# Dilated attention heads: queries and keys kept whole in float32, two heads scored in the row halves of the array, and a first layer that begins with half a modulation chunk

## The chip, the cores and the metric

The kernel runs on one core of a Trainium2 chip. A core has five engines with their own instruction lists: TensorE (matrix products; PE in the profile, its weight loads PEld), VectorE (DVE), ScalarE (ACT), GpSimd (POOL) and SyncE (SP), which here issues all DMA transfers. The time is the device time of the whole program in microseconds (us); three runs of the kernel before took 1956.06, 1959.04 and 1960.41 us, so the median is 1959.04 us.

## What is computed

A two-layer encoder is applied to two groups of tokens, "p" with 512 and "s" with 1024 tokens of width 1024, all in float32. Every layer is RMSNorm, modulation by a shift and a scale that are computed from a conditioning vector, a mixer, RMSNorm, a gate and the residual sum:

```
shift, scale, gate = split(silu(c) @ ada_w + ada_b, 3)
h = rmsnorm(x, pre_g) * (1 + scale) + shift
p = h @ w_in                  # qa ka va ga qb kb vb gb (layer 0)
y = rmsnorm(concat(oa * silu(ga), ob * silu(gb)) @ w_out, post_g)
x = x + gate * y
```

Layer 0 has 8 dense heads ("a") and 8 dilated heads ("b") of 64 channels. A dilated head attends in three patterns, (window, dilation) = (128, 1), (512, 4), (2048, 16), each a sliding window over tokens of one residue; the three outputs are mixed by the softmax of their log sums:

```
for window, dil in ((128, 1), (512, 4), (2048, 16)):
    o, lse = sliding_window(residues(q, dil), residues(k, dil), residues(v, dil), window // (2 * dil))
w = softmax(stack(lse)); out = sum(w * outs)
```

Layer 1 has neighbourhood attention ("c") and a Fourier mixer.

## The kernel before, in words

Tokens go in units of 512: unit 2 is group p, units 0 and 1 are group s. Layer 0 does all of p first, then s; the end of p's layer 0 and the start of its layer 1 are woven into s.

**The planner.** Nobody writes the order of instructions of an engine out by hand. The program states operations on tiles of named pools, with a number of buffers for each; a planner walks through them with a model of the times and puts on each engine, in program order as priority, what has its data and its buffers. The order that results is fixed. On the chip an engine waits at the instruction that is next, even if a later one could go.

**Products.** Projections split both operands into a rounded high part and a low part (hi and lo, type float32r) and add three products (`tok_gemm`, `chan_gemm`; L141 is the helper that issues them). Products of plain float32 are two instructions each in the profile. A product can use a part of the 128 x 128 array: `tile_position=(row, column)`.

**Queries and keys of layer 0.** `s2_0_unit` projects 256 columns at a time, applies the rotary embedding, transposes and spills. `spill_hl` (L399 to L403) writes a high part (ScalarE) and a low part (VectorE) to DRAM, for dense and dilated heads alike; the queries are scaled by 0.125.

**The dilated heads.** `attn_b` calls `attn_b_unit` for each head and each half of 512 queries. A head loads its keys with the high parts on partitions 0 to 63 and the low parts on 64 to 127 (`load_k`, one buffer), and its queries' high and low parts, each copied to both halves (`load_q`). GpSimd adds the two to a float32 query `qf` (L741). For each tile of 128 queries there are two sections of scores in one PSUM bank ("S", two banks): the band, two rounded products over all 128 rows (L141, tiles `qh`, `ql`; two pieces of 128 keys where the tile is the first or last of the group), and the four residue classes modulo 4, float32 products with 32 columns of the array for each class (L769, `qf`). Band and classes are issued for two query tiles before `softmax_b` masks, takes the maximum (L804 or L809), the exponential (L816), and scales (L819), into tiles "e" (four buffers of 1024 columns; a head uses two). Then the transposes, the copies to SBUF, the products with V (L633) and `fold`.

**The beginning.** `run` loads the modulation weights of 512 channels (`ada_w`, four tiles of 512 KB for a chunk), `adaln` multiplies them with the conditioning vector (L222; eight float32 products on 32 columns each), copies, transposes by four small products (`adt`) and adds the bias. The order is: chunk 2 (scale of channels 0 to 511), the four tiles of x of unit 2 and their norm, chunk 0 (shift of the same channels), the weights of job "kva", chunks 3 and 1. `s1_part` builds the modulated operand for 256 channels at a time. The first half of job "kva" (channels 0 to 511) is multiplied before chunks 3 and 1 are; the second half, and all of job "qa0", after them.

Of the kernel before, what the change touches and what calls it, by code (L numbers as in the profile page):

```python
# [18 lines left out]
P = 128  # L19
# [103 lines left out]
class Body:  # L123
# [80 lines left out]
    def ada_w(self, l, c, tag="x", slots=XB):  # L204
        aw = self.a["ada_w"][l].rearrange("(p j) e -> p j e", p=P)
        ws = []
        for j in range(0, KC, 2):
            ws.append(self.sb.tile([P, 2, 512], F32, tag=tag, name=f"aw{l}{c}{j}", bufs=slots))
            self.dma(ws[-1], aw[:, j:j + 2, c * 512:c * 512 + 512])
        return ws  # L210

# [16 lines left out]
    def adaln_end(self, l, c, parts, alloc=None):  # L228
# [14 lines left out]
        pt = (alloc or self.pD)(f"adt{l}{c}")[:, 0:8].rearrange("p (k g) -> p k g", g=2)  # L243
        for k in range(4):
            self.mm(pt[:, k], parts[:, k * P:(k + 1) * P], self.sel, True, True)
        ks = slice(4 * (c % 2), 4 * (c % 2) + 4)
        mod = self.mod[:, l, row, ks, :]
        nc.vector.tensor_add(mod, pt, self.adb[:, l, row, ks].unsqueeze(2).to_broadcast([P, 4, 2]))
        if row == 1:
            nc.vector.scalar_tensor_tensor(mod, mod, 1.0, self.adb[:, l, 2, ks].unsqueeze(2).to_broadcast([P, 4, 2]),  # L250
                                           op0=ALU.add, op1=ALU.mult)
# [95 lines left out]
    def load_w(self, src, name, dve=()):  # L347
# [5 lines left out]
        for c in range(KC // 2):  # L353
# [40 lines left out]
    def spill_hl(self, ps, dst, u, scale, nm, classes=False):  # L394
# [9 lines left out]
        if not classes:  # L404
            self.dma(dst[:, :, u * 512:(u + 1) * 512].rearrange("t p s -> p t s"), st)
            return
        for t in range(2):
            self.dma(dst[t].rearrange("p (r a) -> p r a", r=4)[:, :, P * u:P * u + P],
                     st[:, t].rearrange("p (r a) -> p r a", r=4))
# [62 lines left out]
    def scratch0(self):  # L472
        dr = self.dr
        self.qd, self.kd, self.vd, self.gd, self.md = {}, {}, {}, {}, {}
        for g in self.G:
            n = g.name
            for p in range(8):
                self.qd[0, n, p] = dr.tile([2, P, g.S], F32R, name=f"q0{n}{p}")
            for p in [0, 4, 5, 6, 7]:
                self.kd[0, n, p] = dr.tile([2, P, g.S], F32R, name=f"k0{n}{p}")  # L480
# [10 lines left out]
    def w_0(self, kind, u):  # L491
        base = dict(qa=0, kv=512, ga=768, qb=1280, kb=1792, vb=2304, gb=2816)
        c0 = base[kind[:2]] + (0 if kind == "kva" else 256 * int(kind[2]))
        return self.load_w(self.a["w_in_ab"][0][:, c0:c0 + 256], f"{kind}{u}", W0)
# [15 lines left out]
    def s2_0_unit(self, H, u, w, typ, q, nm):  # L510
# [12 lines left out]
        for jp in range(2):  # L523
            i = 4 * gu + 2 * jp
            ps = self.early.pop((typ, jp), None)
# [25 lines left out]
        def finish():  # L551
            for c in range(1 if typ == "kva" else 2):
# [9 lines left out]
                elif typ == "kb":  # L562
                    self.spill_hl(pt, self.kd[0, n, 4 + 2 * q + c], gu, 1.0, f"{nm}{c}", g.U > 1)
                else:
                    self.spill_hl(pt, self.qd[0, n, 2 * q + c + (4 if typ == "qb" else 0)], gu, 0.125, f"{nm}{c}")
# [139 lines left out]
    def attn_b(self, g, h, quad):  # L705
        for head in range(4 * quad, 4 * quad + 4):
            self.attn_b_unit(g, h, head)
# [23 lines left out]
    def attn_b_unit(self, g, h, head):  # L731
# [3 lines left out]
        pr, hh = 4 + head // 2, head % 2  # L735
        nm = f"b{n}{head}{h}"
# [5 lines left out]
        kf = km.bitcast(F32)  # L742
        if hh == 0:
            self.vt = self.load_vb(g, h, pr, nm)
        V1, V2 = [[t[:, i, HD * hh:HD * hh + HD] for t in ts for i in range(t.shape[1])] for ts in self.vt]
        k4 = km.rearrange("p (r a) -> p r a", r=4)
        es = [pool.tile([P, 1024], F32, tag="e", name=f"e{nm}{i}", bufs=EB) for i in range(2)]
        ev = []
        pss = []
        for t in range(4):  # L750
            tt = 4 * h + t
            qs = slice(t * P, (t + 1) * P)
            ps = self.pS(f"s{nm}{t}")
            pss.append(ps)

            if 0 < tt < NT - 1:
                a0 = 32 * tt - 16
                self.qk(ps[:, 0:256].rearrange("p (j r a) -> p j r a", j=2, r=4), (qh, ql), qs,
                        k4[:, :, a0:a0 + 64].rearrange("p r (j a) -> p j r a", a=32))
            else:  # L760
                for j in range(2):
                    a0 = min(max(32 * (tt + j) - 16, 0), nn - 32)
                    self.qk(ps[:, j * P:(j + 1) * P].rearrange("p (r a) -> p r a", r=4), (qh, ql), qs, k4[:, :, a0:a0 + 32])
            if t % 2 == 0:
                continue

            for t in (t - 1, t):
                for r in range(4):
                    nc.tensor.matmul(pss[t][32 * r:32 * r + 32, 256:256 + nn], qf[:, t * P + 32 * r:t * P + 32 * r + 32],  # L769
                                     kf[:, r * nn:(r + 1) * nn], start=False, stop=True, tile_position=(0, 32 * r),  # L770
                                     skip_group_check=True)
            for t in (t - 1, t):
                ev.append(self.softmax_b(g, pss[t], es[t // 2][:, (t % 2) * 512:(t % 2) * 512 + 256 + nn], 4 * h + t, f"{nm}{t}"))
        po = self.pO(f"o{nm}")

        for gi in range(2):
# [4 lines left out]
            for j, t, cnt, x in ((0, 0, 1, 0), (1, 0, 2, 1), (2, 1, 1, 3)):  # L781
                t += 2 * gi
                self.pv2(po[:, t * P:(t + cnt) * P], V1[2 * gi + j], ph[:, x * P:(x + cnt) * P], j if gi == 0 else 2 + j)
# [9 lines left out]
        of = self.fold(po, nm, view=lambda x: x.rearrange("p (t r a) -> p r t a", t=4, r=4))  # L793
        self.dma(self.md[0, n, pr][HD * hh:HD * hh + HD, 512 * h:512 * h + 512], of)
# [381 lines left out]
    def run(self):  # L1176
# [4 lines left out]
        with tc.tile_pool(name="l0", bufs=1) as self.l0:  # L1181
            H = [], []
            self.dma(self.adb, self.a["mod_b"])
            self.adaln(0, 2, self.ada_w(0, 2, "hl", HB))()
            xs = self.s1_norm(0, 2)
            ws = self.ada_w(0, 0, "hl", HB)
            self.pre["kva"] = self.w_0("kva", 2)
            w3, w1 = self.ada_w(0, 3, "hh", HB), self.ada_w(0, 1, "e", EB)
            self.adaln(0, 0, ws)()
            pts = {k: self.s1_transpose(0, 2, xs, k, f) for k, f in enumerate([self.pS] * SB + [self.pT] * TB)}  # L1190
            self.s1_part(0, 2, xs, H, 2, pts)

            for jp in range(2):
                ps = self.early["kva", jp] = self.pD(f"tkva2{jp}").rearrange("p (t c) -> p t c", t=2)
                self.tok_gemm(ps, H, self.pre["kva"], jp, 0, 4)
            pts = {k + 4: self.s1_transpose(0, 2, xs, k + 4, f) for k, f in enumerate([self.pS] * SB + [self.pT] * TB)}
            self.adaln(0, 3, w3, self.pO)()
            self.adaln(0, 1, w1, self.pO)()
            self.s1_part(0, 2, xs, H, 2, pts)
# [134 lines left out]
```

## Time and profile before

| | us |
|---|---|
| median of three runs (1956.06 to 1960.41) | 1959.04 |
| profiled execution | 1960.37 |
| its span, first to last instruction | 1958.6 |
| TensorE busy | 1892.0 (97%) |
| VectorE busy | 1207.7 (62%) |
| ScalarE busy | 925.5 (47%) |
| GpSimd busy | 625.8 (32%) |

Busy time is the union of an engine's instructions; matrix products overlap in their pipeline, so an instruction's duration is longer than its distance to the next, and the distance is what counts in a dense stretch. The span is cut into 40 slices on the page: TensorE is at 7 tenths in the first one and at 8 or more in all others, and 354.03 MB go through the DMA queues, 181 GB/s on the mean.

### The profile page before, as it was taken

The page shows a single profiled execution, that of the slowest core. Times are in us where ns is not written, and L with a number is a line of the kernel's source. Part 1 is how long each engine was busy: PE and PEld are TensorE (multiplying, and loading weights), DVE is VectorE, ACT ScalarE, POOL GpSimd, SP SyncE. Part 2 cuts the span into 40 slices and gives each one's busy share as a digit, 9 for nine tenths or more (in the row PEclk, how much of TensorE's full clock was granted, in tenths as well). Part 3 has the DMA queues.
Part 4 walks back from the last instruction along what each step waited for, and adds up shares of the span by engine and source line. Part 5 has one row for each costly group of instructions (what it writes and reads, how often), then busy time and mean ns, then how long its engine had stood idle before and what let it go on. Part 6 is the DMA issues. An engine that isn't in the chain of part 4 may idle for free.

```text
span 1958.6 us, 38066 instructions
## 1 busy us (share of the span) xinstructions
PE 1892.0 (97%) x13720; PEld 1630.5 (83%) x13720; DVE 1207.7 (62%) x3131; ACT 925.5 (47%) x2195; POOL 625.8 (32%) x558
## 2 busy tenths in 40 slices
PE   7999999999999999999999999899999999998998
PEld 3889778999999888888986767798887888887898
DVE  2788765354858666767765586564566544668643
ACT  3456544343356554565544454454554333445531
POOL 2832234255622121121111231344433323335320
PEclk8999999999999999999999999999999999999999
DMA  9655564567664432244455585654667664668643
GB/s 337 218 178 162 174 183 154 169 202 226 224 219 140 130 96 87 77 134 139 125 163 167 178 284 163 215 173 138 217 214 231 196 188 142 201 207 263 209 169 140
DMA packets 266493, 354.03 MB, mean 181 GB/s; under 512 B 26568, under 2 KB 173352, under 8 KB 266304
## 3 DMA queue, kind: packets, MB, share of 16 engines
q1 hardware_dynamic: 266304, 351.60, 56.8%
q8 instruction: 108, 1.77, 0.4%
q14 instruction: 81, 0.66, 0.1%
HBM read 263.36 MB, written 88.16 MB: 179 GB/s over the span
## 4 chain that ended last, share of the span: by engine, by line
PE 78%; DMA 9%; DVE 7%; issue 2%; POOL 2%; ACT 1%; SPq 1%; POOLq 0%; ACTq 0%; DVEq 0%
PE y L141 9%; PE c1q L141 5%; PE c1g L141 5%; PE c1k L141 5%; PE t1v L141 5%; PE tvb L141 4%; PE ggb L141 3%; PE gga L141 3%; PE sas L141 3%; PE oas L141 3%; PE ptas L145 3%; PE tqb L141 2%; PE tkb L141 2%; PE tqa L141 2%; PE tkva L141 2%
## 5 line engine op out<-in xcount | busy, mean ns | idle before, releaser
L141 PE MATMUL y<-who,hhm 128*128 128x256 f32 x768 | 218.1, 286 | 4.7 <-ACT hhm L842 4.6
L141 PE MATMUL y<-who,hlm 128*128 128x256 f32 x768 | 216.3, 285 | 3.7 <-DVE hlm L843 3.6
L141 PE MATMUL y<-wlo,hhm 128*128 128x256 f32 x768 | 217.0, 285 | 0.4 <-DVE wlo L358 0.4
L141 PEld LDWEIGHTS y<-who,hhm 128*128 128x128 f32 x768 | 146.1, 191 | 8.4 <-ACT hhm L842 5.7
L141 PEld LDWEIGHTS y<-who,hlm 128*128 128x128 f32 x768 | 146.0, 191 | 7.2 <-DVE hlm L843 5.0
L141 PEld LDWEIGHTS y<-wlo,hhm 128*128 128x128 f32 x768 | 145.9, 191 | 1.7 <-issue 1.0
L680 ACT ACTIVATE eas<-sas,nmas 128x512 f32<-128x512 f32 x128 | 86.9, 684 | 71.0 <-DVE nmas L676 71.0
L1034 POOL TENSOR_TENSOR bics<-TTcs,mkc 128x288 f32<-128x288 f32 (+1 forms) x72 | 65.6, 912 | 128.0 <-DVE mcs L1047 105.6
L617 DVE TENSOR_TENSOR ptlas<-ptas,pthas 128x512 fp32r<-128x512 f32 x128 | 85.6, 684 | 18.3 <-ACT pthas L615 18.0
L671 DVE TENSOR_REDUCE mxas<-sas 128x1 f32<-128x512 f32 x128 | 86.4, 683 | 11.6 <-PE sas L141 10.8
L358 POOL TENSOR_TENSOR wlo<-wso,who 128x512 fp32r<-128x512 f32 x40 | 54.3, 1360 | 98.6 <-ACT who L357 91.7
L615 ACT CAST pthas<-ptas 128x512 fp32r<-128x512 f32 x128 | 70.4, 591 | 32.1 <-PE ptas L145 26.6
L141 PE MATMUL t1v<-wh1v,hl 128*128 128x256 f32 x288 | 82.3, 286 | 0.0
L141 PE MATMUL t1v<-wh1v,hh 128*128 128x256 f32 x288 | 82.0, 285 | 0.0
L141 PE MATMUL t1v<-wl1v,hh 128*128 128x256 f32 x288 | 81.6, 283 | 0.0
L1052 ACT ACTIVATE ecs<-ecs,ngmcs 128x288 f32<-128x288 f32 (+1 forms) x96 | 54.7, 571 | 55.8 <-DVE ngmcs L1050 54.6
L145 PE MATMUL ptas<-ident,eas 128*128 128x128 f32 x512 | 77.1, 272 | 1.5 <-DVE ptlas L617 1.5
L865 ACT ACTIVATE ysq<-y 128x256 f32<-128x256 f32 x96 | 36.7, 383 | 85.2 <-PE y L141 70.0
L141 PE MATMUL oas<-ptlas,Vas 128*128 128x256 f32 x256 | 69.4, 297 | 1.1 <-DVE ptlas L617 1.1
L141 PE MATMUL oas<-pthas,Vas 128*128 128x256 f32 x256 | 69.1, 285 | 0.0
L357 ACT CAST who<-wso 128x512 fp32r<-128x512 f32 x80 | 48.8, 616 | 42.2 <-issue 15.4
L842 ACT CAST hhm<-og 128x512 fp32r<-128x512 f32 x48 | 29.7, 619 | 79.7 <-POOL og L841 44.1
(615 smaller groups left out, 6475.1 us busy)
## 6 DMA issues: line engine op xcount, KB each, us to landing
aw<-ada_w SPq DMA_DIRECT2D x48, 512.0 KB
wso<-w_out_ab SPq DMA_DIRECT2D x48, 256.0 KB
kcs<-k1s SPq DMA_DIRECT2D x24, 384.0 KB
kbs<-k0s SPq DMA_DIRECT2D x16, 512.0 KB
wso<-w_out_cd SPq DMA_DIRECT2D x32, 256.0 KB
ws1k<-w_in_cd SPq DMA_DIRECT2D x28, 256.0 KB
wskb<-w_in_ab SPq DMA_DIRECT2D x24, 256.0 KB
wsqb<-w_in_ab SPq DMA_DIRECT2D x24, 256.0 KB
```

What stands on the lines that cost most here:

```text
L141: self.nc.tensor.matmul(out, l, r, start=start, stop=stop, skip_group_check=True)
L145: self.nc.tensor.transpose(out, in_, self.ident[:k, :k])
L357: nc.scalar.copy(hi, st)
L358: (nc.vector if c in dve else nc.gpsimd).tensor_sub(lo, st, hi)
L615: nc.scalar.copy(h[:rows, :w], pt[:rows, :w])
L617: nc.vector.tensor_sub(lo[:rows, :w], pt[:rows, :w], h[:rows, :w])
L671: nc.vector.tensor_reduce(mx[:, c:c + 1], ps, op=ALU.max, axis=AX.X, negate=True)
L680: nc.scalar.activation(e[:, 512 * c:512 * c + 512], pss[c], AF.Exp, bias=nmx, accum_out=den[:, c:c + 1])
L842: nc.scalar.copy(hh, t)
L865: nc.scalar.activation(sq[:, 0:256], ps[:, t], AF.Square, accum_out=ss[j][:, job:job + 1])
L1034: nc.gpsimd.tensor_add(b, T[:, :, wo:wo + w], self.mcol[:, kind, wo:wo + w].unsqueeze(1).to_broadcast([P, nrow, w]))
L1052: nc.scalar.activation(e, e, AF.Exp, bias=ngm, scale=0.125, accum_out=den)
```

## The change

**Dilated heads.** Their queries and keys are spilled as plain float32 by a new `spill` (one ScalarE operation, one DMA), into DRAM tiles of one part instead of two. `attn_b_unit` becomes `attn_b_pair`: two heads at a time. The keys of both heads are one tile, head 0 on partitions 0 to 63 and head 1 on 64 to 127, and so are the queries; `qf` and its addition are gone. For each query tile the band and the classes of both heads are float32 products over 64 rows, alternating between the heads (`HD * x` is the row); each head has its own S bank. The masks and exponentials of the two heads of a query tile follow its scores, and the pair holds four e tiles. What comes after the exponentials moves to `out_b`, unchanged.

**The beginning.** x is loaded first. `ada_w` can load half a chunk (256 channels, two tiles of 512 KB), and `ada_half` multiplies it. The order is: halves 0 of chunks 2 and 0, the first half of the weights of "kva" and "qa0", halves 1 of both chunks, chunks 3 and 1. After each half 256 channels of the operand are built, and both jobs "kva" and "qa0" multiply them, in four PSUM banks that stay theirs; the second half of their weights and of their products follows after chunks 3 and 1. The columns of the modulation are added in `ada_cols`, which was the end of `adaln_end`.

```diff
+    def ada_half(self, l, c, half, ws, alloc):
+        ps = alloc(f"ada{l}{c}{half}")[:, 0:256]
+        for j in range(KC):
+            q = 32 * (j % 4)
+            nc.tensor.matmul(ps[q:q + 32, :], self.sc[:, j, :], ws[j // 4][:, j % 4], start=(j < 4), stop=(j >= 4),
+                             tile_position=(0, q), skip_group_check=True)
+        parts = self.sb.tile([P, 512], F32, tag="scr", name=f"mod{l}{c}{half}", bufs=SCB)[:, 0:256]
+        nc.scalar.copy(parts, ps)
+        self.ada_cols(l, c // 2, 4 * (c % 2) + 2 * half, 2, parts, alloc)
...
+    def spill(self, ps, dst, u, scale, nm, classes=False):
+        st = self.sb.tile([P, 2, 512], F32, tag="sp", name="sp" + nm, bufs=SPB)[:, 0]
+        self.nc.scalar.mul(st, ps, scale)
+        if classes:
+            dst, st = (x.rearrange("p (r a) -> p r a", r=4) for x in (dst, st))
+            self.dma(dst[:, :, P * u:P * u + P], st)
+        else:
+            self.dma(dst[:, u * 512:(u + 1) * 512], st)
...
-    def attn_b_unit(self, g, h, head):
+    def attn_b_pair(self, g, h, pr):
-        km = self.load_k(self.kd[0, n, pr], HD * hh, S, nm)
-        qh, ql = self.load_q(self.qd[0, n, pr], HD * hh, h, nm)
-        qf = pool.tile([P, 512], F32, tag="qf", name="qf" + nm, bufs=1)
-        nc.gpsimd.tensor_add(qf, qh, ql)
+        km = pool.tile([P, S], F32, tag="k", name="k" + nm, bufs=KB)
+        self.dma(km, self.kd[0, n, pr])
+        q = pool.tile([P, 512], F32, tag="qh", name="q" + nm, bufs=QB)
+        self.dma(q, self.qd[0, n, pr][:, 512 * h:512 * h + 512])
-        es = [pool.tile([P, 1024], F32, tag="e", name=f"e{nm}{i}", bufs=EB) for i in range(2)]
+        es = [[pool.tile([P, 1024], F32, tag="e", name=f"e{nm}{x}{i}", bufs=EB) for x in range(2)] for i in range(2)]
+        rows = [slice(HD * x, HD * x + HD) for x in range(2)]
         for t in range(4):
+            pss = [self.pS(f"s{nm}{t}{x}") for x in range(2)]
...
+            for view, k in parts:
+                for x, rs in enumerate(rows):
+                    nc.tensor.matmul(view(pss[x]), q[rs, t * P:(t + 1) * P], k[rs], start=True, stop=False,
+                                     tile_position=(HD * x, 0), skip_group_check=True)
+            for r in range(4):
+                for x, rs in enumerate(rows):
+                    nc.tensor.matmul(pss[x][32 * r:32 * r + 32, 256:256 + nn], q[rs, t * P + 32 * r:t * P + 32 * r + 32],
+                                     km[rs, r * nn:(r + 1) * nn], start=False, stop=True, tile_position=(HD * x, 32 * r),
                                      skip_group_check=True)
+            for x in range(2):
+                ev[x].append(self.softmax_b(g, pss[x], es[t // 2][x][:, (t % 2) * 512:(t % 2) * 512 + 256 + nn], tt,
+                                            f"{nm}{t}{x}"))
+        for x in range(2):
+            v1, v2 = [[t[:, i, rows[x]] for t in ts for i in range(t.shape[1])] for ts in (V1, V2)]
+            self.out_b(g, h, pr, x, ev[x], v1, v2, f"{nm}{x}")
...
-            self.adaln(0, 2, self.ada_w(0, 2, "hl", HB))()
             xs = self.s1_norm(0, 2)
-            ws = self.ada_w(0, 0, "hl", HB)
-            self.pre["kva"] = self.w_0("kva", 2)
-            w3, w1 = self.ada_w(0, 3, "hh", HB), self.ada_w(0, 1, "e", EB)
-            self.adaln(0, 0, ws)()
...
+            wq = [self.ada_w(0, 2, "e", EB, 0), self.ada_w(0, 0, "e", EB, 0)]
+            weights(range(2))
+            wq += [self.ada_w(0, 2, [("sp", SPB)] * 2, half=1), self.ada_w(0, 0, [("sp", SPB), ("row", RB)], half=1)]
+            w3, w1 = self.ada_w(0, 3, "hh", HB), self.ada_w(0, 1, "hl", HB)
+            pts = {k: self.s1_transpose(0, 2, xs, k, self.pT) for k in range(2)}
+            ps = {(kind, jp): (self.pD if (kind, jp) != ("qa0", 1) else self.pO)(f"t{kind}2{jp}").rearrange(
+                "p (t c) -> p t c", t=2) for kind in W for jp in range(2)}
+            for c in range(2):
+                for i in range(2):
+                    self.ada_half(0, 2 - 2 * i, c, wq[2 * c + i], self.pS)
+                self.s1_part(0, 2, xs, H, 1, pts)
+                for (kind, jp), o in ps.items():
+                    self.tok_gemm(o, H, W[kind], jp, 2 * c, 2 * c + 2)
+                pts = {k: self.s1_transpose(0, 2, xs, k, self.pT) for k in (2 * c + 2, 2 * c + 3)}
+            weights(range(2, 4))
+            self.adaln(0, 3, w3, self.pS)()
+            self.adaln(0, 1, w1, self.pS)()
+            self.s1_part(0, 2, xs, H, 2, pts, alloc=(self.pT, self.pS))
```

## Rows read from the trace of the kernel before

**Rows 1.** The page's totals: busy us, share of span, instructions

```profile
PE 1892.0 (97%) x13720; PEld 1630.5 (83%) x13720; DVE 1207.7 (62%) x3131; ACT 925.5 (47%) x2195; POOL 625.8 (32%) x558
```

**Rows 2.** Busy time by stretch; last columns clock, DMA share, GB/s

```profile
0.00:50.00 50.00, 35.59 (x183) 18.80 (x184) 15.50 (x39) 15.74 (x34) 11.82 (x17) 0.85 0.95 336
...
196.00:309.00 113.00, 109.05 (x896) 84.66 (x894) 74.41 (x294) 53.54 (x121) 35.66 (x27) 0.97 0.55 166
990.00:1230.00 240.00, 235.62 (x1980) 175.46 (x1979) 162.22 (x430) 115.47 (x260) 53.33 (x40) 1.00 0.61 189
```

**Rows 3.** Busy time by stretch, score tiles sbs, then sbp (PE, PEld, DVE)

```profile
990.00:1230.00 240.00, 71.63 (x672) 37.22 (x672) 42.39 (x64) 1.00 0.61 189
...
196.00:309.00 113.00, 30.40 (x352) 20.58 (x352) 18.72 (x62) 0.97 0.55 166
```

**Rows 4.** TensorE's timeline, group s: start us, us, instruction, tiles

```profile
996.71 0.28 PE L141 MATMUL sbs<-kbs,qhbs 128*128 128x256 f32 x1
996.83 0.28 PE L141 MATMUL sbs<-kbs,qlbs 128*128 128x256 f32 x1
997.03 1.07 PE L769 MATMUL sbs<-kbs,qfbs 128*32 128x256 f32 x16
998.04 0.39 PE L141 MATMUL t1v<-wh1v,hl 128*128 128x256 f32 x1
```

**Rows 5.** The same, a second half of a head's work

```profile
1026.35 0.28 PE L141 MATMUL sbs<-kbs,qhbs 128*128 128x256 f32 x1
...
1026.68 0.63 PE L769 MATMUL sbs<-kbs,qfbs 128*32 128x256 f32 x6
1027.24 0.39 PE L141 MATMUL sbs<-kbs,qhbs 128*128 128x256 f32 x1
...
1027.67 1.05 PE L769 MATMUL sbs<-kbs,qfbs 128*32 128x256 f32 x10
```

**Rows 6.** The same, group p

```profile
260.67 0.65 PE L769 MATMUL sbp<-kbp,qfbp 128*32 128x128 f32 x16
261.25 0.66 PE L145 MATMUL pt1bp<-ident,ebp 128*128 128x128 f32 x4
```

**Rows 7.** TensorE's timeline, beginning; in brackets idle time and releaser

```profile
5.69 5.85 PE L222 MATMUL ada<-aw,sc 128*32 128x512 f32 x16 [5.69 <-DMA aw<-ada_w]
...
22.88 1.06 PE L222 MATMUL ada<-aw,sc 128*32 128x512 f32 x8
...
28.09 0.39 PE L141 MATMUL tkva<-whkva,hh 128*128 128x256 f32 x1
...
49.28 0.58 PE L141 MATMUL tkva<-whkva,hh 128*128 128x256 f32 x1 [1.59 <-DVE hh L316]
...
71.14 0.28 PE L141 MATMUL tqa<-whqa,hl 128*128 128x256 f32 x1
```

**Rows 8.** SyncE's queue, first modulation tiles; then busy time of a stretch

```profile
1.64 1.97 SPq L138 DMA_DIRECT2D aw<-ada_w  x4
...
5.00:10.00 5.00, 4.31 (x14) 0.78 (x16) 0.00 (x0) 0.00 (x0) 0.00 (x0) 1.00 1.06 402
```

**Rows 9.** Operations by tile: ns min/median/max, first and last start

```profile
L741 POOL TENSOR_TENSOR qfbs<-qhbs,qlbs x16: 1271/1295/1821, 962.6 to 1213.5; 128x512 f32<-128x512 f32 x16
...
L403 DVE SCALAR_TENSOR_TENSOR spqb<-qTqb,spqb x12: 675/681/692, 149.8 to 659.8; 128x512 fp32r<-128x512 f32 x12
...
L400 DVE TENSOR_TENSOR spkb<-qTkb,spkb x12: 675/681/693, 126.3 to 637.2; 128x512 fp32r<-128x512 f32 x12
```

**Rows 10.** Exponentials by tile; then a VectorE group of 990 to 1230 us

```profile
L816 ACT ACTIVATE ebs<-ebs,ngbs x64: 705/722/740, 994.7 to 1230.2; 128x512 f32<-128x512 f32 x64
...
L819 DVE TENSOR_SCALAR ebs<-ebs,rdbs x64: 462/486/1596, 995.7 to 1231.4; 128x512 f32<-128x512 f32 x64
L804 DVE CUSTOM_DVE_ANT_1 ebs<-sbs,mask_b x56: 675/688/693, 992.7 to 1227.4; 128x512 f32<-128x512 f32 x56
...
L627 DVE COPY ptc2bs<-pt2bs 128x512 f32<-128x512 f32 x15 | 10.3, 688 | 3.3 <-PE pt2bs L145 3.0
```

More of the change, by code (lines that the diff above doesn't have):

```diff
@@ L242, in adaln_end, with ada_cols @@
             return
[L243 to L244 removed]
+        self.ada_cols(l, row, 4 * (c % 2), 4, parts, alloc or self.pD)
+    def ada_cols(self, l, row, k0, nk, parts, alloc):
+        nc = self.nc
+        pt = alloc(f"adt{l}{row}{k0}")[:, 0:2 * nk].rearrange("p (k g) -> p k g", g=2)
+        for k in range(nk):
             self.mm(pt[:, k], parts[:, k * P:(k + 1) * P], self.sel, True, True)
[L246 removed]
+        ks = slice(k0, k0 + nk)
         mod = self.mod[:, l, row, ks, :]
[L248 removed]
+        nc.vector.tensor_add(mod, pt, self.adb[:, l, row, ks].unsqueeze(2).to_broadcast([P, nk, 2]))
         if row == 1:
[L250 removed]
+            nc.vector.scalar_tensor_tensor(mod, mod, 1.0, self.adb[:, l, 2, ks].unsqueeze(2).to_broadcast([P, nk, 2]),
                                            op0=ALU.add, op1=ALU.mult)
@@ L345, in w_pair, with load_w @@
         return [pool.tile(shape, F32R, tag=t, name=f"w{x}{name}", bufs=bufs) for x, t in zip("hl", tags)]
-    def load_w(self, src, name, dve=()):
+    def load_w(self, src, name, dve=(), cs=range(KC // 2)):
         nc, pool = self.nc, self.sb
@@ L352, in load_w @@
         his, los = [], []
-        for c in range(KC // 2):
+        for c in cs:
             st = pool.tile([P, 2, nc_], F32, tag="ws", name=f"ws{name}{c}", bufs=WSB)
@@ L403, in spill_hl @@
             nc.vector.scalar_tensor_tensor(st[:, 1], ps, scale, st[:, 0], op0=ALU.mult, op1=ALU.subtract)
[L404 to L409, printed above, removed]
+        self.dma(dst[:, :, u * 512:(u + 1) * 512].rearrange("t p s -> p t s"), st)
+    def spill(self, ps, dst, u, scale, nm, classes=False):
[6 more added lines that the diff above has]
+            self.dma(dst[:, u * 512:(u + 1) * 512], st)
     def spill_v(self, ps, nh, dst, nm):
@@ L476, in scratch0 @@
             n = g.name
-            for p in range(8):
+            for p in range(4):
                 self.qd[0, n, p] = dr.tile([2, P, g.S], F32R, name=f"q0{n}{p}")
-            for p in [0, 4, 5, 6, 7]:
-                self.kd[0, n, p] = dr.tile([2, P, g.S], F32R, name=f"k0{n}{p}")
+            self.kd[0, n, 0] = dr.tile([2, P, g.S], F32R, name=f"k0{n}0")
+            for p in range(4, 8):
+                self.qd[0, n, p] = dr.tile([P, g.S], F32, name=f"q0{n}{p}")
+                self.kd[0, n, p] = dr.tile([P, g.S], F32, name=f"k0{n}{p}")
             self.vd[0, n, "a"] = dr.tile([g.S, 2, P], F32R, name=f"va0{n}")
@@ L705, in attn_b @@
     def attn_b(self, g, h, quad):
-        for head in range(4 * quad, 4 * quad + 4):
-            self.attn_b_unit(g, h, head)
+        for pr in (4 + 2 * quad, 5 + 2 * quad):
+            self.attn_b_pair(g, h, pr)
     def load_vb(self, g, h, pr, nm):
@@ L1193, in run @@
[L1193 to L1199, printed above, removed]
+            W = {kind: ([], []) for kind in ("kva", "qa0")}
@@ new lines, in weights @@
+            def weights(cs):
+                for kind in W:
+                    if kind == "qa0":
+                        self.wend = [(("qh", "ql"), QB), (("pth", "ptl"), PTB)]
+                    for l, n in zip(W[kind], self.w_0(kind, 2, cs)):
+                        l += n
+                    self.wend = None
+            wq = [self.ada_w(0, 2, "e", EB, 0), self.ada_w(0, 0, "e", EB, 0)]
+            weights(range(2))
+            wq += [self.ada_w(0, 2, [("sp", SPB)] * 2, half=1), self.ada_w(0, 0, [("sp", SPB), ("row", RB)], half=1)]
```

69 lines of the change are left out of this document (31 added, 38 removed).

## The prediction

> **What bounds the kernel now.** I read the page's totals first, then busy time by stretch, then TensorE's timeline inside the two stretches that the change rewrites. TensorE is busy for 97% of the span [rows 1]. In the two stretches in which the dilated heads run it is busy 109.05 of 113 us and 235.62 of 240 us, while VectorE reaches about two thirds and GpSimd less than a third [rows 2]. Between the heads' own instructions stand products of other jobs (gates, projections, the output product), so a head's latency is filled, and the end comes when TensorE's list is done. What shortens that list shortens the run almost one for one; what relieves another engine or a queue is worth nothing until TensorE waits for it. The exception is the first 50 us: TensorE is busy there for only 35.59 us, at a mean granted clock of 0.85 of 2.4 GHz, while the DMA engines move 336 GB/s [rows 2].
>
> The sums are made against the profiled execution, 1960.37 us (span 1958.6 us and 1.8 us around it); the median of the runs is 1959.04 us, so I take 1.3 us off at the end.
>
> **The scores of the dilated heads.** All their score instructions keep TensorE busy for 71.6 us in the 1024-token group and 30.4 us in the 512-token group [rows 3]. There are 8 heads, 4 query tiles of 128 to a half, and 2 halves or 1: per query tile and pair of heads, 32 and 16 in number, that is 2.24 and 1.90 us. I count the change in such steps.
>
> Today a step has two sections. The banded scores are rounded products on the whole array, two (high and low query) for 256 keys; they follow each other at 0.12 us [rows 4]. The class scores are float32 products on 32 columns of the array each. Sixteen instructions, the eight products of two query tiles (a float32 product is two instructions), take 1.01 us at 256 keys and 0.58 us at 128 [rows 4, 6]. Four products on different columns thus run together, and I count waves: a wave is one instruction on each part of the array, 0.25 us for 256 columns and 0.145 us for 128. Changing the array's division costs about 0.1 us each way: 0.20 us between the last whole-array product and the first class product, where 0.12 is usual [rows 4].
>
> After the change both sections are float32 with 64 rows, head 0 on the upper rows, head 1 on the lower. No product in this trace is split by rows, so whether the halves run together as the column parts do has to be bounded.
> - Together everywhere: two waves of banded scores, two of class scores, two changes of division: 0.1 + 0.5 + 0.1 + 0.5 = 1.2 us a step (1.28 for the 8 edge steps, whose band is two pieces of 128 keys: four waves of 0.145). Small group: 0.1 + 0.5 + 0.1 + 0.29 = 0.99 us (edge 1.07). In all 24 x 1.2 + 8 x 1.28 + 8 x 0.99 + 8 x 1.07 = 55.5 us against 102.0: 46 us less.
> - Never together: each section twice, 2.4 and 2.56 us, 1.98 and 2.14 us: 111 us, 9 us more.
>
> Which end is nearer? Four column parts do run as one wave, and nothing in the rows sets rows apart from columns, so I take the hardware to do it. The order of instructions is what I doubt. Engines work in order, and the order was fixed by a planner that starts what has its buffers. There are two score banks. Today two query tiles share them; after the change the two heads of one tile do. The mask-and-maximum that empties a bank takes 0.69 us on VectorE [rows 10], so the second bank comes free that much after the first, and the planner lets the first proceed alone. That is already to be seen: in [rows 5] the first tile's band is followed by six class instructions (three products) before the second tile's band. I counted such a break in 12 of the 16 second halves of the heads' work in this group; the first halves, which find both banks free, are mostly whole, as in [rows 4]. After the change a break means that head 0's band and most of its class products go by without head 1: about two separate sections each, 2.44 and 2.06 us on average, no better than today. The first tile of each pair finds both banks free; of the other three I take three quarters to be broken, as today: 18 of 32 steps and 9 of 16. Then 14 x 1.22 + 18 x 2.44 = 61.0 us, and 7 x 1.03 + 9 x 2.06 = 25.7 us: 86.7 against 102.0, **15 us less**. With all of the other three broken it is 5 us less.
>
> The Trainium skill bears on the price of "together". "TensorE: Matmul & The Clock Gate", section Measured speedup vs the span model, gives 3.07 times for four row parts, so less than their number. The waves of four column parts here come nearer to four: 1.01 us for eight products of 2 x 256 columns [rows 4]. By the page's ratio, which I would put at 1.5 for two halves as an estimate, a paired step would cost about 1.6 instead of 1.2 us and the 15 us would be about 8; no run here shows a row part yet, and my sum goes by the waves.
>
> **What leaves other engines.** The sum that rebuilds the float32 query, 24 times 1.3 us on GpSimd, and 24 subtractions of 0.68 us on VectorE that made the low parts in the spill, go away [rows 9]. Keys are loaded once for a pair, queries once instead of four 64-row copies. All this lies beside a busy TensorE [rows 2]; I count it at nothing, with up to 5 us of gain (there is 4 us of idle TensorE in each of the two stretches) as the bound. Were that cover gone, 16 us of VectorE would be the most it is worth. What is late next is the tile of exponentials: a pair now holds all four, so the next pair's maximum waits until this pair's transposes have read them (the slow rival below).
>
> **The beginning.** TensorE starts at 5.69 us, 4.05 us after the first 512 KB were asked for [rows 7, 8], and the queue then moves 402 GB/s [rows 8], 1.3 us for each such tile. Today the order is 4 modulation tiles of 512 KB, 4 of x, 4 of modulation; the last modulation product of these ends at 23.9 us, and 4.15 us later, after its copy, transposes, additions, the modulated operand and its rounding, the first projection product starts at 28.09 us [rows 7]. After the change 4 tiles of x and 4 of half a modulation chunk suffice: the eighth lands at 5.7 + 7 x 1.3 = 14.8 us, its products take the 1.06 us of [rows 7], and 4.15 us later the first projection product starts, at 20.0: 8.1 us earlier. It is followed by 48 more products (of the first query job), which are taken off the later list, so they cost nothing. What is added is two more modulation products' worth of issue: four halves instead of two wholes, between 0 and 2 x 1.06 us; I take 1. The weights of the second projection job move ahead of mask and tables in the queue; they add 1 MB, 2.6 us, before the last modulations, which today lie landed while TensorE still works through the first products (those start their second half at 49.28 us [rows 7]; 12 MB at 402 GB/s are there by about 34 us). Gain **7 us**. Bounds: all 14.4 us of idle time of the first 50 us, or a loss of 3 us, if the first products find the low clock (0.85 on the mean in this stretch [rows 2]) for longer and the halves cost their full 2 us. The gain carries through, because TensorE is busy nearly all the time from there on.
>
> Sum: 1960.4 - 15 - 7 = 1938; against the median, **1937 us**.
>
> **The rivals.**
> - *Together everywhere.* If the planner puts both heads side by side in every step, 46 and 7 us go: 1907 us. For it: both heads' products stand next to each other in the program. Against: the breaks of [rows 5].
> - *The halves don't run together.* Then the change does not do what it says: 9 us more and 7 us less give 1962 us, within the measurement of no change. For it: no row of the trace shows a row split. The Trainium skill's page "TensorEngine Tiling (Array Packing)", section Key Properties, says that tiles are independent and that a change of division drains the engine; by that the halves run, and the drain is in my 0.1 us.
> - *Slower: four tiles of exponentials.* A pair holds all four, so pairs follow each other in a chain: four steps of 2 x (0.69 + 0.49) us on VectorE, 0.72 us for the last exponential, and eight copies of 0.69 us between the transposes [rows 10], 15.7 us at least. Today a pair's two heads take 240 / 8 = 30 us with what stands between [rows 2], so there is slack of about 14 us. It decides from the point at which waiting in queues doubles the chain, which VectorE at two thirds could do. At 34 us a pair, 8 pairs cost 32 us and 4 small ones some 12: with 7 us gained at the start 1960 + 44 - 7 = 1997 us; at 32 us it is about 1975. Against it: the other jobs' products fill such waits today.
>
> **Chances and range.** Forecast 0.6, with its own range of 1922 to 1952 (5 to 25 us from the scores, 3 to 12 from the start); together everywhere 0.15; halves not together 0.13; chain of exponentials 0.12. The range of 8 in 10 is 1904 to 1959: it takes in the forecast, the first rival down to 3 us beyond its time, and a part of the second. A measurement here tells about 0.2% (4 us) from no change. Faster: 0.6 + 0.15 + 0.03 of the third = 0.78; within 0.2%: 0.10; slower: 0.12.
>
> **What would show it.** Paired steps: float32 products of 64 rows in waves of 0.25 us, with head 0's and head 1's first instructions some hundredths of a microsecond apart; their busy time over both groups 55 us (together), about 87 (forecast) or about 111 (never). Broken steps: class products of one head between the bands of the two. The start: first projection product at about 20 us, end of the first query job some 7 us before today's 71.3 us [rows 7]. The chain: TensorE idle in front of score products that wait for VectorE, and a lower share in 990 to 1230 us. I am wrong in the mechanism if the score time falls and the end does not, or if the start gains more than the scores.

## The result and the profile after

The changed kernel takes 1942.49 us (median of 5 runs, 1940.53 to 1945.32), the kernel before beside it on the same chip 1957.11 us. The ratio is 0.9928, 95% interval 0.9907 to 0.9949: 14 us faster, 10 to 18 by the interval. The forecast was 1937 us, 22 less than before. The profiled execution took 1940.53 us (span 1938.7), 19.9 us less span than that of before. It is the fastest of the five, and the profiled one of before (1960.37 us) is among the slowest of its kind, so accounts from the two traces show some 5 us more than the times do.

The page's totals of the changed kernel, to be set beside [rows 1] (busy us, share of the span, instructions):

```profile
PE 1879.1 (97%) x13752; PEld 1624.4 (84%) x13752; DVE 1186.0 (61%) x3110; ACT 927.1 (48%) x2197; POOL 591.8 (31%) x534
```

Busy time by stretch of the changed kernel, with the columns of [rows 2]; the last two are the stretches from the first to the last score product of a dilated group:

```profile
0.00:50.00 50.00, 34.24 (x257) 24.45 (x257) 14.74 (x42) 19.06 (x40) 17.68 (x22) 0.99 0.92 303
188.00:293.00 105.00, 101.23 (x879) 77.13 (x878) 70.71 (x293) 50.96 (x116) 26.53 (x20) 0.98 0.45 130
968.00:1205.00 237.00, 235.99 (x1981) 171.85 (x1980) 156.80 (x426) 115.58 (x261) 33.02 (x25) 1.00 0.50 155
```

TensorE is still busy for 97%, and in group s for 235.99 of 237 us; GpSimd and the transfers fell and nothing took the room. The score products alone, busy time of TensorE, weight load and VectorE in two stretches that hold all of them (group p, then s), against [rows 3]:

```profile
150.00:330.00 180.00, 25.83 (x352) 13.93 (x352) 19.10 (x64) 0.99 0.47 141
```
```profile
950.00:1260.00 310.00, 64.72 (x672) 26.11 (x672) 42.50 (x64) 0.99 0.51 160
```

TensorE's timeline of the changed kernel, group s: first a whole step at 968.95 (an edge step, whose band is two pieces), the last line being the next job; then a broken one from 1001.03:

```profile
968.95 0.72 PE L791 MATMUL sbs<-kbs,qbs 64*128 64x128 f32 x8
969.60 0.66 PE L796 MATMUL sbs<-kbs,qbs 64*32 64x256 f32 x16
970.19 0.50 PE L141 MATMUL c1q<-hh,wh1q 128*128 128x512 f32 x1
...
1001.03 0.70 PE L791 MATMUL sbs<-kbs,qbs 64*128 64x256 f32 x2
1001.65 0.62 PE L796 MATMUL sbs<-kbs,qbs 64*32 64x256 f32 x4
1002.21 0.66 PE L662 MATMUL obs<-ptc2bs,V2bs 128*64 128x128 f32 x8
...
1003.82 0.70 PE L791 MATMUL sbs<-kbs,qbs 64*128 64x256 f32 x2
1004.44 0.65 PE L796 MATMUL sbs<-kbs,qbs 64*32 64x256 f32 x12
1005.02 0.39 PE L141 MATMUL t1v<-wh1v,hl 128*128 128x256 f32 x1
```

Whole: both heads' band and class products in 0.65 + 0.59 = 1.24 us. Broken: head 0's band and two of its class products in 1.18 us, and after another job head 1's band and the other six in 1.20 us. Sixteen class instructions of two heads took 0.59 us from their first start to the start of the next job, four took 0.56 and twelve 0.58: the length of such a stretch hardly depends on how many parts of the array work in it.

The busy time of a group of instructions says more than it costs: an instruction ends after the next one has started (0.66 us busy, 0.59 to the next start). For the accounts below I took from the trace, for each TensorE instruction, the time to the next one's start, at most its own length (its slot), and called the rest idle. In slots the scores of both groups fell from 94.8 to 85.9 us, and TensorE's idle time after the first product from 51.8 to 41.3. All slots together are the page's busy time, in which the overlaps are counted once: 1892.0 and 1879.1 us. The first product comes 3.3 us later.

The beginning of the changed kernel, TensorE's timeline (against [rows 7]):

```profile
8.99 0.69 PE L145 MATMUL xt<-ident,x 128*128 128x128 f32 x2 [8.99 <-DVE x L310]
...
11.69 1.08 PE L221 MATMUL ada<-aw,sc 128*32 128x256 f32 x8 [0.33 <-DMA aw<-ada_w]
...
18.63 1.02 PE L141 MATMUL adt<-sel,mod 128*128 128x2 f32 x4 [0.81 <-ACT mod L224]
20.81 1.08 PE L221 MATMUL ada<-aw,sc 128*32 128x256 f32 x8 [1.16 <-DMA aw<-ada_w]
21.82 1.97 PE L145 MATMUL xt<-ident,x 128*128 128x128 f32 x8
23.44 0.56 PE L141 MATMUL tkva<-whkva,hh 128*128 128x256 f32 x1
```

and, of the same kernel, ScalarE's rounding that makes the first operand:

```profile
20.80 0.62 ACT L340 CAST hh<-xm 128x512 fp32r<-128x512 f32 x1
```

The operand is there at 21.42 us. But a quarter chunk of the second half's modulation (the row of 20.81, for whose transfer TensorE waited 1.16 us) and eight transposes stand ahead of the projection in TensorE's order, so it starts at 23.44.

### The profile page after: what moved, and what is told of

It reads as the page before. It is cut to its first block, busy times and chain, and to the rows that moved or that the text cites. A ratio compares the mean times of both kernels' runs of the same rounds, so it can differ in the third digit from the quotient of the medians.

```text
span 1938.7 us, 37892 instructions
## 1 busy us (share of the span) xinstructions
PE 1879.1 (97%) x13752; PEld 1624.4 (84%) x13752; DVE 1186.0 (61%) x3110; ACT 927.1 (48%) x2197; POOL 591.8 (31%) x534
## 4 chain that ended last, share of the span: by engine, by line
PE 47%; DMA 4%; DVE 2%; issue 1%; ACT 0%; POOL 0%; SPq 0%; POOLq 0%; ACTq 0%; DVEq 0%
PE y L141 10%; PE t1v L141 5%; PE c1g L141 5%; PE c1q L141 5%; PE c1k L141 5%; PE ocs L662 2%; PE ptcs L145 2%; PE obs L662 2%; PE sbs L791 1%; PE sbs L796 1%; PE scs L141 1%; PE oas L141 1%; PE c1d L141 1%; DMA og<-g1s 1%; PE pt1bs L145 1%; PE ocp L662 1%
## 5 line engine op out<-in xcount | busy, mean ns | idle before, releaser
L644 ACT CAST pthas<-ptas 128x512 fp32r<-128x512 f32 x128 | 70.6, 590 | 29.2 <-PE ptas L145 25.7
L1086 ACT ACTIVATE ecs<-ecs,ngmcs 128x288 f32<-128x288 f32 (+1 forms) x96 | 54.7, 571 | 56.9 <-DVE ngmcs L1084 55.5
```

The source lines that it names most:

```text
L644: nc.scalar.copy(h[:rows, :w], pt[:rows, :w])
L1086: nc.scalar.activation(e, e, AF.Exp, bias=ngm, scale=0.125, accum_out=den)
```

## The experiments

Theory A, from the prediction: TensorE's list sets the end, a paired step costs 1.2 us and a broken one double, and each slot saved is saved from the time. Its rivals: the halves don't run together, or a chain of other engines sets the pace of the heads.

**1. The heads alone**, with the beginning of before:

```diff
-            wq = [self.ada_w(0, 2, "e", EB, 0), self.ada_w(0, 0, "e", EB, 0)]
-            weights(range(2))
...
+            self.adaln(0, 2, self.ada_w(0, 2, "hl", HB))()
             xs = self.s1_norm(0, 2)
+            ws = self.ada_w(0, 0, "hl", HB)
...
```

> The dilated heads of the changed kernel with the beginning of the kernel before. Theory A (TensorE's list of instructions is the bound, so its time is what counts): the score products fall from 94.8 us to 85.9 us of TensorE's time, by the distance from each to the next instruction in the two traces, so about 9 us less than before, and up to 5 more where a load or a subtraction that is gone held TensorE up: ratio to before 0.993 to 0.996. Theory B (what counts is the lighter load on the queue, VectorE and GpSimd): all of the gain of the changed kernel but the beginning's, also 7 to 13 us; this run alone does not part the two, the next two do. If the beginning made the whole gain, the ratio is 1.000.

Ratio 0.997 (0.9958 to 0.9983), by which it takes 5.9 us less than before. Score slots fell by 8.8 us; about 3 of them were lost again in slots of other products (the heads' own transposes +2.1, a query projection +1.8), and idle time stayed (51.8 to 51.1).

**2. The beginning alone**, with the heads of before (`attn_b_unit` and both parts of queries and keys):

```diff
-        for pr in (4 + 2 * quad, 5 + 2 * quad):
-            self.attn_b_pair(g, h, pr)
+        for head in range(4 * quad, 4 * quad + 4):
+            self.attn_b_unit(g, h, head)
...
```

> The beginning of the changed kernel with the dilated heads of the kernel before. Theory A: the modulation products take 6.1 us less of TensorE's time, and at equal amounts of TensorE work the changed kernel was 8.4 us ahead when the first dilated scores began, so 7 to 9 us less than before, ratio 0.9955. If the head start is given back later to a wait that does not move (the first keys' round trip through DRAM, the tables of the second group), the ratio is 0.998 to 1.000.

Ratio 0.9984 (0.9973 to 0.9995), by which it takes 3.1 us less, under the 7 to 9 expected. In its profile the first dilated score of group p comes at 188.4 us, 8.1 earlier than before, and the first one of group s at 982.2, 8.8 earlier, so the beginning gives what it was to give and the lead holds that far. The last score of s comes at 1221.5 us, only 4.7 earlier: between the two TensorE idles for 6.9 us instead of 4.4, and the same products take 1.6 us more in slots. By the end of the span 5.7 us are left. Why the lead shrinks there no run shows. The two parts alone add to 9.0 us, both together gave 14; the intervals (3.3 to 8.2, 1.0 to 5.3, 10 to 18) don't exclude that they simply add.

**3. Apart**: head 0's band and classes, then head 1's.

```diff
-            for view, k in parts:
-                for x, rs in enumerate(rows):
+            for x, rs in enumerate(rows):
+                for view, k in parts:
...
-            for r in range(4):
-                for x, rs in enumerate(rows):
+                for r in range(4):
```

> The changed kernel, but with the loop over the two heads outside: head 0's band and classes, then head 1's, so that no product of one row half has the other half beside it. Transfers, banks and the work on VectorE, ScalarE and GpSimd are the same. By the planned order there are 139 sections of scores in the larger group and 66 in the smaller, where the changed kernel has 103 and 49; at 0.63 us a band section, 0.56 and 0.34 us a class section that is 114 us instead of 86. Theory A: 28 us more than the changed kernel, about 1971 us, slower than the kernel before. Theory B: within 5 us of the changed kernel.

Ratio 1.0011 (0.9993 to 1.0029): 17 us slower than the changed kernel by the medians (1959.6), 23 by the spans. Its score products, TensorE busy time first, in the stretches of above:

```profile
150.00:330.00 180.00, 34.90 (x352) 18.61 (x352) 20.43 (x64) 0.97 0.44 129
```
```profile
950.00:1260.00 310.00, 85.91 (x672) 33.63 (x672) 44.04 (x64) 1.00 0.48 148
```

120.8 us against 90.6; in slots 115.6 against 85.9, where 114 was expected. One head's class products, eight instructions, take 0.57 us from start to next start, where sixteen of two heads took 0.59:

```profile
994.36 0.64 PE L794 MATMUL sbs<-kbs,qbs 64*32 64x256 f32 x8
994.93 0.70 PE L791 MATMUL sbs<-kbs,qbs 64*128 64x256 f32 x2
```

The same products in the same number cost 30 us more because they don't meet: the halves do run together. Of the 28 us that were expected in time, 17 came; some of the rest is seen elsewhere (idle time fell by 4.7 us, slots of the output product by 3.9). By Theory B, the lighter load on the queue, VectorE and GpSimd, this run would have stayed within 5 us of the changed kernel: it is out as the whole cause.

**4. Together**: after a query tile's softmax, VectorE rewrites one column of the next tile's query from 0 times the maximum of head 1. The next tile's scores so wait until both banks are read, and both heads start side by side.

```diff
+            if t < 3:
+                c = (t + 1) * P
+                nc.vector.scalar_tensor_tensor(q[:, c:c + 1], self.mxb, 0.0, q[:, c:c + 1], op0=ALU.mult, op1=ALU.add)
...
+        self.mxb = mx[:, 0:1]
```

> The changed kernel, but each query tile's scores of both heads wait for the maximum of both heads of the tile before: one small VectorE operation adds zero times that maximum to the first column of the next tile's queries (values unchanged). Then both score banks are free when the planner begins a tile, and it puts the heads side by side: 67 sections in the larger group and 37 in the smaller instead of 103 and 49, 59 us of TensorE's time instead of 86. Theory A: 27 us less than the changed kernel, about 1915 us. Theory B: no change, or a little slower by the 36 added operations. The rival of the four tiles of exponentials: the gain stays under 10 us, and TensorE shows idle time before score products that wait for VectorE.

Score slots fell as expected, by 25.6 us to 60.3. The time did not: ratio 0.9929 (0.9911 to 0.9948), the changed kernel's own. Idle time rose by 22.5 us to 63.8, and the slots of all other products by 7.6 (the output product's by 4.8). Busy time by stretch, the changed kernel (columns as in [rows 2]):

```profile
960.00:1080.00 120.00, 119.98 (x952) 88.29 (x950) 75.23 (x200) 55.94 (x122) 14.34 (x11) 1.00 0.45 137
1080.00:1160.00 80.00, 79.00 (x653) 56.11 (x651) 57.52 (x151) 42.11 (x95) 16.30 (x12) 1.00 0.64 205
1160.00:1260.00 100.00, 91.83 (x815) 79.02 (x813) 61.13 (x148) 46.67 (x124) 23.61 (x24) 0.97 0.51 162
```

and "together":

```profile
960.00:1080.00 120.00, 120.00 (x971) 90.36 (x970) 74.35 (x213) 58.01 (x126) 15.13 (x12) 1.00 0.46 142
1080.00:1160.00 80.00, 66.26 (x614) 51.59 (x612) 57.13 (x143) 37.89 (x90) 17.16 (x12) 0.94 0.63 200
1160.00:1260.00 100.00, 83.63 (x778) 72.14 (x775) 60.57 (x157) 44.58 (x113) 19.16 (x22) 0.90 0.47 147
```

Up to 1080 us nothing is lost: by the count of TensorE's instructions other than scores, "together" leads by 10.0 us at 1046 us, and by nothing at 1240. In between TensorE stands still, and its granted clock falls to 0.94 and 0.90 as well. TensorE's waits from 960 to 1260 us (us in total, times, longest), first the changed kernel's longest:

```profile
PE y L141 <- ACT hhm L876: 5.6, 1, 5.6
```

then those of "together", of which the last is the added wait itself:

```profile
PE y L141 <- ACT hhm L880: 14.2, 2, 10.0
PE sbs L791 <- DMA kbs<-k0s: 7.4, 3, 4.5
PE y L141 <- POOL wlo L378: 3.4, 1, 3.4
...
PE sbs L791 <- DVE qbs L804: 0.4, 1, 0.4
```

and two of them in its timeline:

```profile
1084.27 0.39 PE L141 MATMUL c1d<-hh,wl1d 128*128 128x512 f32 x1
1089.14 0.70 PE L791 MATMUL sbs<-kbs,qbs 64*128 64x256 f32 x4 [4.48 <-DMA kbs<-k0s]
...
1240.73 0.58 PE L141 MATMUL y<-who,hhm 128*128 128x256 f32 x1 [9.95 <-ACT hhm L880]
```

At 1084.27 us the last projection (c1d) that needs nothing of the heads has run; in the changed kernel all of these products (12.47 us of busy time) still lie between 1080 and 1120 us. From here on, as I read these waits, a pair's chain is bare: its keys, for which there is one place, then scores, softmax and outputs, and last the way of the outputs through memory to the operand of the output product. The tiles of exponentials are in this chain too. VectorE waits for the transposes to free them, in the changed kernel (first line) and in "together" (second); in the kernel before it has no such wait in this stretch:

```profile
DVE ebs L838 <- PE pt2bs L145: 12.1, 5, 4.3
DVE ebs L841 <- PE pt2bs L145: 15.2, 6, 3.6
```

In the changed kernel TensorE has other products for this time. Theory A held while there was something to fill with. I call the corrected one A': a saved slot is worth its time only as long as other products last.

**5. Together in group p alone.**

```diff
-            if t < 3:
+            if t < 3 and n == "p":
```

> The changed kernel with the wait of e4 (the next query tile's scores start only when both heads' sums of the tile before are read) in group p alone; group s scored as in the changed kernel. In the order of TensorE's instructions group p has 37 stretches of score products of one division in place of 49. Theory A (TensorE's list sets the end; what is saved is kept wherever other products are left to fill the waits): score slots of p 24.6 to about 19.0 us as in e4, idle time of TensorE within 2 us of the changed kernel's 41.3, time 4 to 6 us under the changed kernel's, ratio to the kernel before 0.9900 to 0.9910. Rival (the added wait gives back in p too what it saves): ratio 0.9925 to 0.9935, idle time up by 4 us or more.

Ratio 0.9884 (0.9862 to 0.9905), 1936.36 us, 6.1 us under the changed kernel by the medians (3.6 by the profiled executions). Slots of p fell by 5.6 us, idle time rose by 2.5. In group p, where over 600 us of other work follow before the next dilated head, the slots are kept.

**6. Together in p and in the first half of s.**

```diff
-            if t < 3:
+            if t < 3 and h == 0:
```

> The wait of e4 in group p and in the first half of group s's queries (the first 16 of its 32 query tiles of a pair of heads); the second half as in the changed kernel. Stretches of one division: 37 in p (49), 87 in s (103). Theory A' (TensorE's list bounds until the other products run out, about two thirds into group s's attention; after that the chain of key load, scores, exponentials and output does): score slots 85.9 to about 71, and because the second half is not slowed the idle time rises by under 6 us, not by 22 as in e4; time 8 to 14 us under the changed kernel's, 1929 to 1935, ratio 0.986 to 0.989. Rival (the work left to fill is used up earlier by just as much, so the loss comes back in the second half): idle time up by 10 us or more, ratio 0.991 to 0.994.

Ratio 0.989 (0.987 to 0.991), 1937.25 us: no better than 5, though the score slots are 9.0 us fewer than there. Idle time rose from 43.8 to 49.9, and what opened lies between 1080 and 1160 us again (first line, TensorE busy for 72.02 of 80 us); its waits, same view as in 4:

```profile
1080.00:1160.00 80.00, 72.02 (x621) 51.98 (x620) 56.79 (x141) 36.99 (x87) 14.28 (x11) 0.94 0.59 191
...
PE y L141 <- ACT hhm L880: 9.2, 2, 6.2
PE sbs L791 <- DMA kbs<-k0s: 5.0, 2, 4.3
```

Neither side's numbers were met in full: idle time rose by 8.6 us against the changed kernel, where A' had under 6 and the rival 10 or more; the ratio is at the edge of A', the time outside it. Against 5, the 9.0 us of score slots came back as 6.1 us of idle time and 3.1 us in other products' slots. So for s the rival has the better of it: what is saved early in s uses up the filling products earlier, and is paid back.

**7. Experiment 4 with a second place for the keys of s.**

```diff
-        km = pool.tile([P, S], F32, tag="k", name="k" + nm, bufs=KB)
+        if n == "s" and pr % 2 == 0:
+            km = self.l0.tile([P, S], F32, tag="rope", name="k" + nm, bufs=1)
+        else:
+            km = pool.tile([P, S], F32, tag="k", name="k" + nm, bufs=KB)
```

> e4 (the wait in both groups) with a second place for the keys of group s's pairs, so that a pair's keys load while the pair before is scored. Stretches of one division in s: 77 (67 in e4, 103 in the changed kernel). Theory A' (in e4's last third the key load of about 5 us a pair stands open on TensorE): the 7.4 us that score products of s waited for keys in e4 are gone, idle time 63.8 to 52 to 57, score slots up by about 5 us against e4's 60.3, time 1936 to 1941, ratio 0.989 to 0.992. Rival (the chain through VectorE, exponentials and output is the slow one and the key load lies beside it): idle time within 3 us of 63.8, time as e4 or slower, ratio 0.992 to 0.996.

Ratio 0.9918 (0.9897 to 0.9938), 1942.88 us, not to be told from 4. The waits for keys are gone and idle time is 57.1, just above the 52 to 57 of A'. But the score slots are 67.8 us, 7.5 more than in 4 where about 5 were expected, and that takes the 6.7 us of idle time back. The next links are late too, in the same view:

```profile
PE y L141 <- ACT hhm L883: 11.7, 2, 10.3
PE sbs L794 <- DVE mxbs L844: 4.9, 3, 2.8
PE y L141 <- POOL wlo L378: 4.2, 1, 4.2
```

Score products now wait for the maximum, the output product as before. So the key load was one link of the chain, and to remove it brought nothing, in part because the second place changes the order of the scores as well (77 stretches of one division in s for 67). That the key load alone held the end, as my part of A' had it, is not shown.

**8. The second place for keys alone**, in the changed kernel: the diff of 7 without that of 4.

> The changed kernel with a second place for the keys of group s's pairs and no added wait. Stretches of one division in s: 116 in place of 103, because one pair's products now also stand between the other's. Theory A (TensorE's list bounds here): the earlier keys buy nothing, the 13 stretches more cost 13 by 0.58 us, score slots up by 7 to 8 us, time 5 to 8 us over the changed kernel's, ratio 0.9955 to 0.997. Rival (the key loads of the 8 pairs bound group s's attention in the changed kernel too): time 5 us or more under it, ratio below 0.990.

Ratio 0.9952 (0.9936 to 0.9968), 1949.16 us: 6.7 us slower than the changed kernel by the medians (all five runs lie above its five, though the two intervals overlap) for 7.4 us more of score slots. Keys earlier bought nothing; a second pair's products between the first pair's broke more steps.

**9. Together in p and in the first two pair passes of s.**

```diff
-            if t < 3:
+            if t < 3 and (n == "p" or (h == 0 and pr < 6)):
```

> The wait of e4 in group p and in the first two of the eight pair passes of group s (two of four pairs, first half of the queries), which lie before the stretch where idle time opened in e4 and e6. Stretches of one division in s: 95 (103 in the changed kernel, 87 in e6). Theory A' (saved slots are kept while other products fill the waits, and what is used up early is missing in the last third): score slots of s fall by another 4 us against e5's; if the fill lasts, the time is 4 us under e5's 1936, 1930 to 1934, ratio to the kernel before 0.985 to 0.9875, idle time within 2 us of e5's 43.8. Rival (every wait added in s is paid back in the last third, however early it stands, because the same filling products are then missing there): time 1935 to 1939, idle time up by 3 us or more against e5's.

Ratio 0.9861 (0.9841 to 0.988), 1934.05 us, the fastest median, and with 5 faster than both kernels. Idle time is 44.7 us, within 2 us of that of 5, as A' had it. Against 5 it is not settled: the intervals overlap, the profiled span is 1 us longer (1935.8), and 2.9 us of score slots saved in s stand against 2.7 more in the output product.

## Why the prediction came out as it did

**The bound** was read rightly for the changed kernel and too simply for what lies beyond it. Where slots were added (experiments 3 and 8) or saved in p (5), time followed, by 0.6 to 1.1 us for each; the 25.6 us of experiment 4 brought nothing. That was my own sign of a wrong mechanism, the score time falling and the end not; for the change itself experiment 1 has both falling.

**The price of a step** is right: 1.24 us for the whole edge step shown where I had 1.28, 2.38 in the two halves of a broken one where I had 2.44. So is the share of broken steps: the order of instructions of the changed kernel has 103 stretches of one division in s and 49 in p. Whole steps would have 64 and 32, a broken one has two more: 19.5 and 8.5 breaks, where I took 18 and 9. The sums of 61.0 and 25.7 us were met by slots of 61.4 and 24.6. Some of this is luck: I carried a share over from a kernel that fills its two banks otherwise. (Its trace has 13 such breaks in the 16 second halves, not the 12 of my count, and 5 of the 16 first halves are cut by other jobs.) That the banks make the breaks is borne out by experiment 4: where both have to be read first, 67 and 37 stretches are left.

**The step that failed is what I subtracted this sum from:** the 102.0 us of [rows 3] are busy time, and my model counted from start to start. In slots the scores before took 94.8 us; [rows 4] shows it, 1.07 us busy and 1.01 to the next start, and [rows 6], 0.65 and 0.58. The term was 15 us and measured 8.9 (8.8 with the heads alone, of which 5.9 reached the end). The gain was forecast 8 us too high, 22 against 14, and this term alone was 6 too high.

**The Trainium skill's ratio.** Head 0's and head 1's first products of a section start 7 to 14 ns apart, and sixteen instructions cost 0.59 us where eight of one head cost 0.57: 1.9 times for two halves. My estimate of 1.5 from the Trainium skill, "TensorE: Matmul & The Clock Gate", section Measured speedup vs the span model, would have made a whole step 1.6 us; the trace has 1.24, and the measurement decides.

**The beginning.** 7 us forecast; 8.1 of lead at the first dilated score (experiment 2), 3.1 by the ratio at the end. The first projection product came at 23.44 instead of 20.0: its operand was there 1.4 us later than I had it, and the other 2.0 us are TensorE's order, which put a wait for a transfer ahead of it. That it led by 8 all the same (my sign for it, the end of the first query job, comes 8.6 us earlier, at 62.8 us) I had not worked out that way: in the first 50 us the granted clock is 0.99 where it was 0.85, with TensorE busy for 34.24 instead of 35.59 us. The projections follow each other at 0.12 us from 25 us on; in the kernel before it was 0.21 until 35 us. There the clock had fallen to 0.50, the lower level of 1.2 GHz, in two stretches (columns as in [rows 2]):

```profile
15.00:20.00 5.00, 4.02 (x13) 1.63 (x13) 3.12 (x10) 2.36 (x8) 1.66 (x3) 0.50 1.05 385
...
30.00:35.00 5.00, 5.00 (x18) 3.11 (x19) 2.97 (x3) 1.21 (x2) 2.88 (x3) 0.50 0.94 310
```

In the 5 us before each, TensorE had been busy for 2.59 and 3.02 us. I had taken the lead to carry through to the end; by experiment 2 it holds to the heads of s and shrinks there, and the cause of that stays open.

**Other engines' relief** was put at nothing, and nothing more is to be seen: GpSimd is busy 34 us less and 21 MB fewer are moved, but with the heads alone TensorE's idle time fell by only 0.7 us (experiment 1), and keys still earlier give nothing (8). No run has the relief without the new scores, so a small gain is not excluded.

**The rivals.** *Together everywhere*: its price for the scores was nearly met in experiment 4 (60.3 us in slots against 55.5), its 1907 us were 36 us off, because the end no longer follows the list. *Halves not together* fell with experiment 3. *Four tiles of exponentials*: VectorE does wait for them in the changed kernel, 12.1 us in five times, but TensorE does not, with 235.99 of 237 us busy, so it cost nothing there. Its kind, a pair's chain that TensorE must wait for, is what met experiments 4 and 7. TensorE's own waits there name keys, maxima and the outputs' way back; how much of the chain's length is VectorE's wait for these tiles (15.2 us in 4) no run separates. I had it slower than before where it only ate the gain.

## What to carry to other kernels

Set a sum's two sides up in the same measure: a model that counts from start to start is compared with starts, not with the busy time of a part of the instructions, which counts tails that lie under the next one. Products on parts of the array pay when both parts are issued side by side, so look at the order first: which bank comes free when decides whether a pair stays whole. And before shortening a list that fills an engine, count the independent work left beside the chain: once that runs out (at 1084 us in experiment 4), what is saved turns into waits.

## What was not expected of the hardware

A stretch of class products of the changed kernel takes 0.56 us with four instructions and 0.59 with sixteen (rows of 1001.65 and 969.60); what is paid for is the stretch. TensorE kept the full clock in a beginning that works less (granted clock 0.99 for 34.24 us busy, 0.85 for 35.59 [rows 2]), its first products now being transposes from 8.99 us on instead of modulation products from 5.69; which of the differences does it, no run here separates.
